# Wider products for retention's keys and values and for gated values with attention's keys and values

## The chip, the cores and the metric

The kernel runs on one core of one Trainium2 chip. The time is the device time of one execution in microseconds (us). Before the change the median of three runs is 982.75 us (982.4 to 984.82). One execution was profiled: it took 980.64 us.

The engines go by the profile's names: PE is the matrix engine (PEld its weight loads), DVE the vector engine, ACT the scalar engine, POOL the GpSimd engine, SP the engine that issues most DMAs.

## The reference, cut to what matters

Two layers of width 1024 over a sequence of 1024. Each layer normalises its input, multiplies it by one wide matrix, splits the result among three groups of heads, and multiplies their outputs by a second matrix:

```python
h = rms_norm(x, pre_gain) * (1.0 + scale) + shift
proj = h @ w_in                       # 1024 x 3088
(aq, ak, av, ag, rq, rk, rv, rg, gq, gk, gv, gg, ga) = jnp.split(proj, IN_SPLITS, axis=-1)
a_out = sliding_window_attention(rotary(aq), rotary(ak), av, sinks) * silu(ag)
r_out = rms_norm(retention(rotary(rq), rotary(rk), rv)) * silu(rg)
g_out = rms_norm(gated_linear_attention(gq, gk, gv, log_a(ga))) * silu(gg)
y = concatenate([a_out, r_out, g_out]) @ w_out
x = x + gate * rms_norm(y, post_gain)
```

Retention's queries, keys, values and gate (rq, rk, rv, rg) have 256 columns each; so have gated attention's values and gate (gv, gg), its queries and keys together (gqk), and attention's keys and values together (kv). Attention's queries and gate have 512 each.

## The kernel before

**Products.** A number is held as two parts, a high and a low one (fp32r), so a product of h with a weight unit takes three passes (high x high, low x high, high x low) over the 8 blocks of 128 rows: 24 matmuls into one bank of PSUM (`accum`). In `project` the stationary operand is a tile of h (128 positions of the sequence) and the moving one is a weight unit of 256 columns (272 for gg, with ga): the result has positions on partitions. In `project_T` and `project_P` it is the other way round: 128 columns of weights are stationary and positions stream, 512 (half of the sequence, from two places, joined by `both`) or 256 (a pair of tiles). The output projection (`y_half`) already streams two weight units joined by `both`, 512 columns in one matmul.

The tag "mm" has three PSUM banks for products (`mm()`, MMB = 3), the other five ("aux") are for the work of cores. A product of 256 columns uses half of a bank.

**Weights.** A weight unit is 256 columns of w_in (or w_out). It is loaded in four pieces of 256 KB into staging tiles ("st", five of them, issued on SP), and each piece is split into its two parts in one of seven places ("arena"): high parts by DVE for the first piece and by ACT for the rest, low parts by DVE and for the last piece by POOL. `PLACE` says which unit goes to which place in which layer, `load` requests a unit as soon as the unit ahead of it in its place has had its last product. `SW` gives places for the last layer's output weights.

**The order on PE** is written out at build time. `layer` runs the products one after another: the two gates (gg, rg), retention (`ret_q` for queries, `project` for keys and values), then `do_gqk`, `do_gv` and `do_kv`, then attention's queries (`attn_rot`) and gates, then the output projection. Everything else is a job, a generator that sleeps for an estimated latency (the table L, in us; a key with "@1" holds for layer 1) on a modelled clock `clk`, which each matmul advances by its columns / 2400 us. `pump` inserts jobs that are due; it is called in `accum` after every 7 matmuls, or every 4 where the result is written as two parts (`len(dst.shape)` of 3), and after each product. PE runs exactly the order so made, and waits where an operand is late. The order on the other engines comes from a scheduler.

**Retention.** `ret_q` for a pair of tiles p makes two products (c = 0, 1) of 256 positions in the two halves of one bank; DVE reads the bank five times (lines 1284 to 1291) and adds (1295). `ret_k` rotates a tile's keys by five operations of DVE (`rotary`, lines 944 to 949), values are multiplied by a decay (line 1658). `ret_core` is the job of one tile: it sleeps rc1, transposes the keys, awaits the queries, sleeps rc2, makes scores, sleeps rc3, then makes the output and carries the state stR to the next tile. A pair's order is: queries, keys of two tiles, values of two tiles; a core is created with the values.

**Gated attention and attention's keys.** `gla_core` (one job for a pair) needs queries, keys and the values of two tiles; `attn_kv` (one job for a tile) rotates and transposes attention's keys. `do_gv` and `do_kv` make their products separately.

The jobs of the gates are `gla_logits` and `gla_log`. The modulation of later stages (`mod_third`) runs as a job beside all this: DVE accumulates 16 tiles of 256 KB a third, each fetched by a DMA (line 317).

## Time and profile before

| what | value |
|---|---|
| median of 3 runs | 982.75 us |
| profiled execution | 980.64 us |
| its span, first to last instruction | 978.5 us |
| granted PE clock | 0.996 |
| matmuls | 7228 |
| of them 128x256 of "mm" with two arena operands | 2304 |
| DMA | 150.34 MB, mean 154 GB/s |

Stages by the order of PE's instructions: preparation and first gate product to 47 us, gates to 88 us, retention of layer 0 to 177 us, gated attention and attention's keys to 285 us, attention's queries and gates and the output projection to 512 us; in layer 1 gates to 562 us, retention to 652 us, gated attention and attention's keys to 757 us, the rest to the end.

A row of a group has line, engine, operation, output<-input, shape and count, then busy time in us, mean duration in ns, and the idle time ahead of it with what ended it. A row of instructions in order of time has start and duration in us. PE's matmuls overlap, so the duration of one is longer than the distance between two starts.

### The profile page before, as it was taken

Reading aid. Unit: us, or ns where it says so; the run is one execution under the profiler, and the core shown is the slowest. Engines: PE = TensorE matmul, PEld = TensorE weight load, DVE = VectorE, ACT = ScalarE, POOL = GpSimd, SP = SyncE. Lnnn points to the kernel's source line nnn. Section 1 sums busy time; section 2 is a strip of 40 time slices with the busy share of each in tenths; the row PEclk is TensorE's granted clock in tenths of the full one; section 3 lists DMA queues with packets and bytes.
Section 4 is the critical chain, followed back from the end, with each engine's and each line's share of the span. In section 5 each row is a group of like instructions: output and inputs, shape, how many; then the busy total and the mean of one; then the engine's idle time right before and its main releaser. Section 6 shows DMA issues by size and latency. Waiting matters only on the chain.

```text
span 978.5 us, 19647 instructions
## 1 busy us (share of the span) xinstructions
PE 958.2 (98%) x7228; PEld 825.8 (84%) x7228; DVE 678.2 (69%) x1598; ACT 395.6 (40%) x1112; POOL 247.7 (25%) x311
## 2 busy tenths in 40 slices
PE   7999999999999999999999999999999999999996
PEld 5799999889998777778889999988999877777875
DVE  6586768678675877645696466785765577677885
ACT  4674102233323656623355420133333257664231
POOL 3431111323310425410133100123332034544000
PEclk9999999999999999999999999999999999999998
DMA  9856315443243345587564121342132434389783
GB/s 353 295 176 197 114 42 150 134 125 103 88 119 118 119 148 184 167 279 242 203 230 152 60 87 33 119 150 62 63 97 77 129 92 135 108 265 282 246 281 121
DMA packets 107532, 150.34 MB, mean 154 GB/s; under 512 B 11142, under 2 KB 58536, under 8 KB 106412
## 3 DMA queue, kind: packets, MB, share of 16 engines
q1 hardware_dynamic: 96140, 134.75, 43.8%
q10 hardware_dynamic: 11296, 14.34, 4.1%
q8 instruction: 57, 0.93, 0.4%
q14 instruction: 39, 0.32, 0.1%
HBM read 110.25 MB, written 36.70 MB: 150 GB/s over the span
## 4 chain that ended last, share of the span: by engine, by line
PE 89%; DVE 6%; DMA 1%; POOL 1%; issue 1%; ACT 1%; SPq 0%; POOLq 0%; DVEq 0%; ACTq 0%
PE mm L170 67%; PE aux L170 18%; PE aux L185 4%; POOL sm L606 1%; DMA ms<-in_w_mod_dram 1%; DMA t<-in_x_dram 0%; DVE t L1288 0%; DVE t L1290 0%; SPq L866 0%; PE mm L185 0%; DVE t L1179 0%; POOL mx L1211 0%; DVE acc L317 0%; DVE t L1099 0%; DVE t L1291 0%
## 5 line engine op out<-in xcount | busy, mean ns | idle before, releaser
L170 PE MATMUL mm<-arena,arena 128*128 128x256 f32 (+2 forms) x1824 | 298.2, 316 | 2.7 <-DVE arena L156 1.4
L170 PE MATMUL mm<-arena 128*128 128x256 f32 (+2 forms) x1728 | 284.7, 318 | 0.0
L170 PEld LDWEIGHTS mm<-arena,arena 128*128 128x128 f32 x1824 | 252.6, 189 | 28.0 <-issue 7.9
L170 PEld LDWEIGHTS mm<-arena 128*128 128x128 f32 x1728 | 240.3, 189 | 24.3 <-issue 4.2
L606 POOL TENSOR_TENSOR sm<-sm,mhalf 128x1 f32<-128x1 f32 (+1 forms) x64 | 57.7, 901 | 292.6 <-DVE sm L603 153.8
L170 PE MATMUL mm<-arena,mx 128*128 128x512 f32 (+1 forms) x564 | 130.9, 388 | 0.0
L170 PEld LDWEIGHTS mm<-arena,mx 128*128 128x128 f32 x564 | 101.5, 188 | 24.0 <-issue 2.3
L154 ACT ACTIVATE t<-aux 128x256 f32<-128x256 f32 (+2 forms) x124 | 52.4, 438 | 97.3 <-PE aux L185 84.6
L154 ACT ACTIVATE arena<-st 128x512 fp32r<-128x512 f32 x94 | 56.1, 628 | 49.4 <-PE mm L170 20.3
L498 POOL TENSOR_TENSOR arena<-st,arena 128x512 fp32r<-128x512 f32 x32 | 45.7, 1429 | 97.5 <-ACT arena L154 81.1
L1049 POOL TENSOR_TENSOR smx<-smx,sm 128x512 f32<-128x512 f32 x32 | 35.0, 1094 | 124.8 <-DVE sm L1048 110.6
L498 DVE TENSOR_TENSOR arena<-st,arena 128x512 fp32r<-128x512 f32 x76 | 59.2, 799 | 3.1 <-ACT arena L154 1.6
L1045 ACT ACTIVATE smx<-smx,sm 128x129 f32<-128x129 f32 x128 | 49.9, 392 | 27.5 <-DVE sm L1042 27.3
L317 DVE SCALAR_TENSOR_TENSOR acc<-ms,c_act,acc 128x512 f32<-128x512 f32 x60 | 45.0, 749 | 17.1 <-DMA ms<-in_w_mod_dram 16.6
L1093 ACT ACTIVATE t<-aux 128x256 f32<-128x256 f32 x32 | 12.3, 383 | 77.3 <-PE aux L170 73.8
L170 PEld LDWEIGHTS aux<-t,mx 32*128 32x128 f32 (+1 forms) x896 | 39.8, 187 | 3.8 <-issue 1.7
L170 PE MATMUL aux<-t,mx 32*128 32x32 f32 (+1 forms) x896 | 40.9, 272 | 0.0
L1040 DVE COPY_PREDICATED smx<-c_masks,aux 128x256 f32<-128x256 int32 x64 | 25.3, 446 | 17.9 <-ACT smx L154 14.5
L1395 DVE SCALAR_TENSOR_TENSOR t<-t,sm,t 128x512 f32<-128x512 f32 x32 | 24.2, 780 | 18.4 <-DMA t<-in_x_dram 12.3
L185 PE MATMUL aux<-c_early,t 128*128 128x128 f32 x186 | 33.8, 277 | 1.5 <-ACT t L1225 0.9
L170 PEld LDWEIGHTS aux<-kT,mx 64*128 64x128 f32 x384 | 24.6, 185 | 10.9 <-issue 7.1
L1098 DVE TENSOR_TENSOR t<-aux,sm 128x256 f32<-128x256 f32 x32 | 13.6, 424 | 27.4 <-POOL sm L606 27.4
(264 smaller groups left out, 1426.9 us busy)
## 6 DMA issues: line engine op xcount, KB each, us to landing
st<-in_w_in_dram SPq DMA_DIRECT2D x96, 256.0 KB, 3.8
ms<-in_w_mod_dram SPq DMA_DIRECT2D x64, 256.0 KB, 3.7
mx<-mixS SPq DMA_DIRECT2D x20, 512.0 KB, 5.6
st<-in_w_last_dram SPq DMA_DIRECT2D x36, 256.0 KB, 3.3
wm<-in_w_m_dram SPq DMA_DIRECT2D x8, 1024.0 KB, 16.7
mixS<-t SPq DMA_DIRECT2D x40, 128.0 KB, 2.1
t<-in_x_dram SPq DMA_DIRECT2D x18, 256.0 KB, 5.0
mixS<-t ACTq DMA_DIRECT2D x32, 128.0 KB, 2.1
```

The source lines that it names most:

```text
L154: A.activation(dst, src, AF.Copy)
L170: T.matmul(dst, lhsT, rhs, start=start, stop=stop)
L185: T.transpose(dst, src, idn)
L317: V.scalar_tensor_tensor(acc, wt, c_act[:, k:k + 1], acc, ALU.mult, ALU.add)
L498: e.tensor_tensor(lo, st, f(hi), ALU.subtract)
L606: G.tensor_tensor(r, r, mhalf[:, :w], ALU.pow)
L1040: V.copy_predicated(sv, curmask.unsqueeze(1).to_broadcast((P, 2, P)), pv[:, :, n // P - 1, :])
L1045: A.activation(sm[:, h, :], sm[:, h, :], AF.Exp, bias=mx[:, h:h + 1], accum_out=sums[:, h:h + 1])
L1049: eng("pn").tensor_tensor(sm[:, :, 0:128], sm[:, :, 0:128], rs.unsqueeze(2).to_broadcast((P, 4, P)), ALU.mult)
L1093: A.activation(sq, po, AF.Square)
L1098: V.tensor_tensor(h4(g1), h4(po), r.unsqueeze(2).to_broadcast((P, 4, 64)), ALU.mult)
L1395: V.scalar_tensor_tensor(xt[j], yg[j], r, xt[j], ALU.mult, ALU.add)
```

## The change

1. Retention's keys and values of a tile become one product: a new `project_2` streams both weight units (512 columns) past the stationary tile of h. The core of a tile is created right after it, and its first sleep, rc1, is 4.5 in both layers (0.8 and 0.0 before).
2. Gated values and attention's keys and values of a tile become one product in the same way (`do_gvkv`).
3. Retention's queries are made by halves of the sequence with `project_T`, two products of 512 positions per half, each with its own bank; `project_P` goes.
4. Units that are streamed together have to lie in places of one arena, so `PLACE` and `SW` change, and with them the order of loads: rk is loaded early where rq was, rq after gg, rv after rg; gqk after the second half's queries; gv and kv together after retention; aq1 after the last of the joint products; the output units o2 and o3, and in the last layer W00 against ag1, change their order.
5. The gates' order: the last pair of gg one place earlier in both layers.

```diff
-SW = dict(W00=6, T1=3, W11=4, W10=5, T2=2, T3=0, T4=1)
+SW = dict(W00=5, T1=3, W11=4, W10=6, T2=2, T3=0, T4=1)
...
-    PLACE.append(dict(gg=_w, rg=5, rq=6, rk=_w, rv=5, gqk=6, gv=_w, kv=5, aq0=6, aq1=_w, ag0=5, ag1=_w,
+    PLACE.append(dict(gg=_w, rg=6, rk=5, rq=_w, rv=6, gqk=_w, gv=5, kv=6, aq0=_w, aq1=5, ag0=6, ag1=_w,
...
+    def project_2(pm, l, t, w0, w1):
+        await_flag(("hT", l, t))
+        c = slice((t % 2) * P, (t % 2) * P + P)
+        h = hT[(l, t // 2)]
+        accum(pm.rearrange("p (s n) -> p s n", s=2), lambda a, k: h[:, a, k, c],
+              lambda b, k: both(w0[:, b, k, 0:256], w1[:, b, k, 0:256]))
...
+    def ret_q(l, hf, w):
+        rqT[hf] = gp.tile([P, NT * P], F32, tag=f"kT{hf}", name=nm("rq"), bufs=1)
+        sn, cs = (tab[:, i, 512 * hf:512 * hf + 512] for i in range(2))
         for c in range(2):
+            pm = mm()
+            project_T(pm, l, hf, w, c * P)
+            u, x = t2(), t2()
+            for b in range(4):
...
+            V.tensor_tensor(u, pm, cs, ALU.mult)
+            V.tensor_tensor(rqT[hf][:, 512 * c:512 * c + 512], u, x, ALU.add)
+            pump()
...
-                load(l, "rk" if name == "gg" else "rv")
+                load(l, "rq" if name == "gg" else "rv")
...
-            for name, p in (("rg", 0), ("rg", 1), ("gg", 2), ("rg", 2), ("gg", 3), ("rg", 3)):
+            for name, p in (("rg", 0), ("rg", 1), ("gg", 2), ("gg", 3), ("rg", 2), ("rg", 3)):
                 do_gates(name, p)
                 if name == "rg" and p == 0:
-                    load(l, "rq")
+                    load(l, "rk")
         else:
-            for ps_ in ((0, 1, 2), (3,)):
-                for name in ("gg", "rg"):
-                    for p in ps_:
-                        do_gates(name, p)
+            for name, ps_ in (("gg", (0, 1, 2)), ("rg", (0, 1)), ("gg", (3,)), ("rg", (2, 3))):
+                for p in ps_:
+                    do_gates(name, p)
...
+        for t in range(NT):
+            if t % 4 == 0:
+                ret_q(l, t // 4, used(l, "rq"))
+                if t:
+                    load(l, "gqk")
+            pm = mm()
+            project_2(pm, l, t, used(l, "rk"), used(l, "rv"))
+            k = ret_k(t, pm[:, 0:256])
+            v = t1()
+            V.tensor_tensor(h4(v), h4(pm[:, 256:512]), vdec.unsqueeze(2).to_broadcast((P, 4, 64)), ALU.mult)
+            job(ret_core(l, t, k, v))
             pump()
...
+        load(l, "gv")
+        load(l, "kv")
...
+        def do_gvkv(p):
+            if p == 0:
+                new_kv()
             for t in (2 * p, 2 * p + 1):
                 pm = mm()
-                project(pm[:, 0:256], l, t, used(l, "gv"))
+                project_2(pm, l, t, used(l, "gv"), used(l, "kv"))
                 vs[t] = t1()
                 copy("gv", vs[t], pm[:, 0:256])
                 if t % 2:
                     job(gla_core(l, p, qks[p], (vs[t - 1], vs[t])))
...
+                job(attn_kv(l, t, pm[:, 256:512]))
                 pump()
 
         do_gqk(0, 0)
         do_gqk(0, 1)
-        do_gv(0)
         do_gqk(1, 0)
-        do_gv(1)
+        do_gvkv(0)
         do_gqk(1, 1)
-        do_gv(2)
-        do_kv(0)
-        do_gv(3)
         for p in range(1, NP_):
-            do_kv(p)
+            do_gvkv(p)
+        load(l, "aq1")
         load(l, "ag0")
...
-                        load(l, ("o3", "ag1")[g])
+                        load(l, ("ag1", "o2")[g])
...
-                        load(l, "o2")
+                        load(l, "o3")
...
-        load(l + 1, "rq")
+        load(l + 1, "rk")
```

More of the change, by code (lines that the diff above doesn't have):

```diff
@@ L594, in project_T @@
               lambda b, k: both(h0[:, b, k, :], h1[:, b, k, :]))
-    def project_P(pm, l, p, w, c):
-        h = hT[(l, p)]
-        accum(pm, lambda a, k: w[:, a, k, c:c + P], lambda b, k: h[:, b, k, 0:256])
+    def project_2(pm, l, t, w0, w1):
[4 more added lines that the diff above has]
+              lambda b, k: both(w0[:, b, k, 0:256], w1[:, b, k, 0:256]))
     def rstd_of(ss, w, scale, eps):
@@ L1271, in gla_out @@
         yield from head_norm_gate(l, t, po, gate, 1.0 / 64.0, EPS, 6)
-    def ret_q(l, p, w):
-        pm = mm()
+    def ret_q(l, hf, w):
+        rqT[hf] = gp.tile([P, NT * P], F32, tag=f"kT{hf}", name=nm("rq"), bufs=1)
+        sn, cs = (tab[:, i, 512 * hf:512 * hf + 512] for i in range(2))
         for c in range(2):
-            project_P(pm[:, 256 * c:256 * c + 256], l, p, w, c * P)
-        def two(x):
-            return x.rearrange("p (c n) -> p c n", c=2)
-        sn, cs = (tab[:, i, 256 * p:256 * p + 256].unsqueeze(1).to_broadcast((P, 2, 256)) for i in range(2))
-        u, x = t2(), t2()
-        for b in range(4):
-            r = slice(32 * b, 32 * b + 32)
-            o = two(x)[32 * (b ^ 1):32 * (b ^ 1) + 32]
-            if b % 2:
-                V.scalar_tensor_tensor(o, two(pm)[r], -1.0, sn[r], ALU.mult, ALU.mult)
-            else:
-                V.tensor_tensor(o, two(pm)[r], sn[r], ALU.mult)
-        V.tensor_tensor(two(u), two(pm), cs, ALU.mult)
-        if p % 2 == 0:
-            rqT[0] = gp.tile([P, NT * P], F32, tag=f"kT{p // 2}", name=nm("rq"), bufs=1)
-        q = rqT[0][:, 512 * (p % 2):512 * (p % 2) + 512]
-        V.tensor_tensor(q, u, x, ALU.add)
-        flag(("rq", l, p), L["rq1"])
-        return two(q)
-    rqT = [None]
+            pm = mm()
+            project_T(pm, l, hf, w, c * P)
+            u, x = t2(), t2()
+            for b in range(4):
+                r = slice(32 * b, 32 * b + 32)
+                o = x[32 * (b ^ 1):32 * (b ^ 1) + 32]
+                if b % 2:
+                    V.scalar_tensor_tensor(o, pm[r], -1.0, sn[r], ALU.mult, ALU.mult)
+                else:
+                    V.tensor_tensor(o, pm[r], sn[r], ALU.mult)
+            V.tensor_tensor(u, pm, cs, ALU.mult)
+            V.tensor_tensor(rqT[hf][:, 512 * c:512 * c + 512], u, x, ALU.add)
+            pump()
+        for p in (2 * hf, 2 * hf + 1):
+            flag(("rq", l, p), L["rq1"])
+    rqT = [None, None]
     def ret_k(t, src):
@@ L1304, in ret_k, with ret_core @@
         return r
-    def ret_core(l, t, q, k, v):
+    def ret_core(l, t, k, v):
         yield lat("rc1", l)
@@ L1314, in ret_core @@
         yield (0.0, ("rq", l, t // 2))
-        qT = q[:, :, P * (t % 2):P * (t % 2) + P]
+        qT = rqT[t // 4].rearrange("p (c n) -> p c n", c=2)[:, :, P * (t % 4):P * (t % 4) + P]
         yield lat("rc2", l)
@@ L1641, in layer @@
         await_flag("tab")
-        for p in range(NP_):
-            last = p == NP_ - 1
-            q = ret_q(l, p, used(l, "rq"))
-            pump()
-            if last:
-                load(l, "gqk")
-            ks = {}
-            for name in ("rk", "rv"):
-                w = used(l, name)
-                for tt in range(2):
-                    t = 2 * p + tt
-                    pm = mm()
-                    project(pm[:, 0:256], l, t, w)
-                    src = pm[:, 0:256]
-                    if name == "rv":
-                        v = t1()
-                        V.tensor_tensor(h4(v), h4(src), vdec.unsqueeze(2).to_broadcast((P, 4, 64)), ALU.mult)
-                        job(ret_core(l, t, q, ks[tt], v))
-                    else:
-                        ks[tt] = ret_k(t, src)
-                    pump()
-                if last:
-                    load(l, {"rk": "gv", "rv": "kv"}[name])
+        for t in range(NT):
[9 more added lines that the diff above has]
+            job(ret_core(l, t, k, v))
+            pump()
+        load(l, "gv")
+        load(l, "kv")
         G.memset(stC, 0.0)
@@ L1683, in do_gqk @@
                 load(l, "aq0")
-        def do_gv(p):
+        def do_gvkv(p):
+            if p == 0:
+                new_kv()
             for t in (2 * p, 2 * p + 1):
                 pm = mm()
-                project(pm[:, 0:256], l, t, used(l, "gv"))
+                project_2(pm, l, t, used(l, "gv"), used(l, "kv"))
                 vs[t] = t1()
@@ L1692, in do_gv @@
                     job(gla_core(l, p, qks[p], (vs[t - 1], vs[t])))
-                pump()
-            if p == NP_ - 1:
-                load(l, "aq1")
-        def do_kv(p):
-            if p == 0:
-                new_kv()
-            for t in (2 * p, 2 * p + 1):
-                pk = mm()
-                project(pk[:, 0:256], l, t, used(l, "kv"))
-                job(attn_kv(l, t, pk))
+                job(attn_kv(l, t, pm[:, 256:512]))
                 pump()
@@ L1756, in layer @@
                 if hf:
-                    if l == DEPTH - 1 and g == 0:
+                    if l == DEPTH - 1 and g:
                         sw_first("W00")
                     else:
-                        load(l, ("o3", "ag1")[g])
+                        load(l, ("ag1", "o2")[g])
         for hf in range(2):
@@ L1827 @@
 EN = {"shw0": "V", "shw1": "A", "shw2": "A", "shw3": "A", "slw0": "V", "slw1": "G", "slw2": "V", "slw3": "G", "sht2": "A", "sht3": "A", "sht4": "A", "slt2": "V", "slt3": "G", "slt4": "G", "sd": "V", "mh0": "A", "mh1": "A", "mh2": "A", "mh3": "A", "mf": "A", "ms0": "V", "ms1": "V", "ms2": "V", "ms3": "V", "yg0": "V", "yg1": "V", "ml0": "V", "ml1": "V", "ml2": "V", "ml3": "V", "mod0": "A", "mod1": "V", "qst": "S", "smh": "A", "sml": "S", "sm0": "S", "sm1": "S", "lao": "S", "sao": "S", "lmix": "S", "ssg": "S", "lsg": "S", "ssr": "S", "lsr": "S", "lx": "S", "sx": "A", "lw": "S", "lwm": "S", "whi0": "V", "whi1": "A", "whi2": "A", "whi3": "A", "wlo0": "V", "wlo1": "V", "wlo2": "V", "wlo3": "G", "xn0": "V", "xn1": "V", "hlo0": "V", "hlo1": "V", "rot0": "V", "rot1": "V", "rdec": "V", "kslo": "V", "qslo": "V", "vlo": "G", "kT": "A", "qT": "A", "sprev": "A", "pn": "G", "pf0": "A", "aoc": "A", "hng": "V", "mh": "A", "gso": "V", "mg": "V", "mgl": "V", "rT": "A", "rv": "A", "gv": "A", "gk": "A", "ak0": "V", "ak1": "V", "ak2": "V", "ak3": "V", "kd0": "G", "kd1": "G", "kd2": "G", "kx1": "G", "kx2": "G", "kx3": "V", "kx4": "V", "qb": "G", "stx": "V"}
-L = {"tt6": 3.0, "sw1": 0.45, "ld1": 1.34, "ld2": 1.2, "ld1@1": 1.35, "ld2@1": 1.31, "swW00": 0.0, "swT1": 0.0, "swW11": 0.34, "swW10": 0.4, "tt1": 16.0, "tt2": 1.62, "tt3": 0.84, "tt4": 1.15, "rq1": 6.5, "pf3": 3.0, "pf4@2": 4.2, "pf4@3": 7.0, "pf5": 0.9, "mod1": 4.6, "mod2": 3.86, "mod3": 12.15, "mod4": 6.79, "mod5": 3.18, "mod6": 9.21, "pre1": 7.44, "kv1": 3.56, "kv2": 5.4, "aq1": 6.0, "aq7": 6.12, "ag1": 6.23, "aq2": 2.4, "aq6": 5.2, "aq3": 10.48, "aq4": 7.36, "aq5": 4.92, "hn1": 8.56, "hn2": 2.85, "gz1": 10.94, "gz2": 9.73, "gl1": 2.76, "gd3": 16.72, "gc1": 0.81, "gc2": 1.64, "gc3": 1.94, "gc4": 1.17, "gc6": 1.32, "gc5": 1.06, "rc1": 0.8, "rc2": 2.64, "rc3": 5.87, "rc4": 4.72, "fin1": 6.58, "lay1": 1.0, "gc4@1": 1.09, "mod2@1": 4.0, "mod3@1": 15.1, "mod5@1": 3.36, "mod6@1": 4.11, "pre1@1": 7.83, "kv1@1": 3.37, "kv2@1": 5.28, "aq1@1": 4.66, "aq7@1": 5.28, "ag1@1": 7.05, "aq2@1": 0.82, "aq6@1": 6.35, "aq3@1": 11.11, "aq4@1": 5.23, "aq5@1": 5.22, "hn1@1": 7.81, "hn2@1": 2.85, "gz1@1": 13.93, "gz2@1": 10.64, "gl1@1": 4.6, "gd3@1": 15.9, "gc1@1": 0.31, "gc2@1": 1.94, "gc3@1": 1.33, "gc6@1": 0.86, "gc5@1": 0.94, "rc1@1": 0.0, "rc2@1": 0.87, "rc3@1": 2.72, "rc4@1": 2.98, "fin1@1": 4.28, "lay1@1": 1.54}
@@ new lines @@
+L = {"tt6": 3.0, "sw1": 0.45, "ld1": 1.34, "ld2": 1.2, "ld1@1": 1.35, "ld2@1": 1.31, "swW00": 0.0, "swT1": 0.0, "swW11": 0.34, "swW10": 0.4, "tt1": 16.0, "tt2": 1.62, "tt3": 0.84, "tt4": 1.15, "rq1": 6.5, "pf3": 3.0, "pf4@2": 4.2, "pf4@3": 7.0, "pf5": 0.9, "mod1": 4.6, "mod2": 3.86, "mod3": 12.15, "mod4": 6.79, "mod5": 3.18, "mod6": 9.21, "pre1": 7.44, "kv1": 3.56, "kv2": 5.4, "aq1": 6.0, "aq7": 6.12, "ag1": 6.23, "aq2": 2.4, "aq6": 5.2, "aq3": 10.48, "aq4": 7.36, "aq5": 4.92, "hn1": 8.56, "hn2": 2.85, "gz1": 10.94, "gz2": 9.73, "gl1": 2.76, "gd3": 16.72, "gc1": 0.81, "gc2": 1.64, "gc3": 1.94, "gc4": 1.17, "gc6": 1.32, "gc5": 1.06, "rc1": 4.5, "rc2": 2.64, "rc3": 5.87, "rc4": 4.72, "fin1": 6.58, "lay1": 1.0, "gc4@1": 1.09, "mod2@1": 4.0, "mod3@1": 15.1, "mod5@1": 3.36, "mod6@1": 4.11, "pre1@1": 7.83, "kv1@1": 3.37, "kv2@1": 5.28, "aq1@1": 4.66, "aq7@1": 5.28, "ag1@1": 7.05, "aq2@1": 0.82, "aq6@1": 6.35, "aq3@1": 11.11, "aq4@1": 5.23, "aq5@1": 5.22, "hn1@1": 7.81, "hn2@1": 2.85, "gz1@1": 13.93, "gz2@1": 10.64, "gl1@1": 4.6, "gd3@1": 15.9, "gc1@1": 0.31, "gc2@1": 1.94, "gc3@1": 1.33, "gc6@1": 0.86, "gc5@1": 0.94, "rc1@1": 4.5, "rc2@1": 0.87, "rc3@1": 2.72, "rc4@1": 2.98, "fin1@1": 4.28, "lay1@1": 1.54}
```

## The prediction

> **What bounds the kernel now.** I read the page first (busy time, clock, the chain that ended last), then what PE waited for, then its groups by shape, then its instructions in order of time at the places that the change touches.

> ```profile
> span 978.5 us, 19647 instructions
> PE 958.2 (98%) x7228; PEld 825.8 (84%) x7228; DVE 678.2 (69%) x1598; ACT 395.6 (40%) x1112; POOL 247.7 (25%) x311
> PEclk9999999999999999999999999999999999999998
> PE 89%; DVE 6%; DMA 1%; POOL 1%; issue 1%; ACT 1%; SPq 0%; POOLq 0%; DVEq 0%; ACTq 0%
> ```

> PE is busy throughout at the full granted clock, and 89% of the chain that ended last is PE. The next view says that almost nothing stops it. It lists what PE's matmuls waited for (total us, times, longest):

> ```profile
> PE mm L170 <- DVE arena L156: 1.4, 1, 1.4
> PE mm L170 <- DVE t L1291: 1.3, 1, 1.3
> ...
> PE aux L185 <- ACT t L1225: 0.9, 2, 0.5
> ```

> The first two lie in the retention stage, the third in gated attention; the other waits of PE are under 0.7 us in sum there, or lie in the first 61 us, ahead of anything that changes. So the time is the length of PE's stream: how many matmuls at what spacing, plus the few waits. The change must act on one of these two.

> **The stream: what is removed and added.** The groups by shape give the counts (times, mean ns):

> ```profile
> L170 PE MATMUL mm<-arena,arena 128*128 128x256 f32 x1152 | 150.6, 285 | 2.7 <-DVE arena L156 1.4 <-DVE t L1291 1.3
> L170 PE MATMUL mm<-arena 128*128 128x256 f32 x1152 | 150.1, 285 | 0.0
> L170 PE MATMUL mm<-arena,arena 128*128 128x512 f32 x480 | 122.3, 402 | 0.0
> L170 PE MATMUL mm<-arena 128*128 128x512 f32 x480 | 122.1, 401 | 0.0
> ```

> A product is 24 matmuls (3 passes over 8 blocks). Per layer, retention's queries are 4 x 2 products of 256 columns, its keys and values 8 tiles x 2, gated values and attention's keys and values 8 x 2: 40 products. In two layers that is 80 x 24 = 1920 of the 2304 matmuls of 128x256; the other 384 are the retention gates (8 x 24 x 2). They become 960 matmuls of 128x512. The streamed columns stay the same, 1920 x 256; 960 matmuls and 960 weight loads go. The means of 285 and 401 ns are no price, since matmuls overlap. The price is the distance between starts in a stretch that nothing interrupts:

> ```profile
> 544.11 5.77 PE L170 MATMUL mm<-arena,arena 128*128 128x256 f32 x48
> 549.72 3.16 PE L170 MATMUL mm<-arena 128*128 128x272 f32 x24
> 552.71 0.39 PE L170 MATMUL aux<-gaT,gwt 128*128 128x512 f32 x1
> ...
> 556.16 5.91 PE L170 MATMUL mm<-arena,arena 128*128 128x256 f32 x48
> 561.91 5.92 PE L170 MATMUL mm<-arena 128*128 128x256 f32 x48
> 567.67 0.99 PE L170 MATMUL mm<-arena,arena 128*128 128x256 f32 x7
> ```

> Start to start, 48 matmuls of 256 columns took 5.61, 5.75 and 5.76 us: 116.9, 119.8 and 120.0 ns each. The third stretch is a product of retention's queries. For 512 columns the nearest rows are pieces of the chain (start, us) of the output projection, which has the new form (weights of two places streamed past a stationary tile), and of attention's queries, which have the form that retention's queries get; then two rows of the last layer:

> ```profile
> 480.71 11.15 PE mm L170 x48
> ```

> ```profile
> 761.51 15.64 PE mm L170 x68
> ```

> ```profile
> 942.80 5.76 PE L170 MATMUL mm<-arena,mx 128*128 128x512 f32 x24
> 948.40 2.96 PE L170 MATMUL mm<-arena,a 128*128 128x512 f32 x12
> ```

> These are 232.3, 230.0 and (5.60 us for 24) 233.3 ns. Two narrow matmuls against one wide one:

> - queries: 192 pairs (2 layers x 4 x 24) x (240.0 - 230.0) = **1.9 us** saved;
> - the rest: 768 pairs x (2 x 118.35, the middle of 116.9 and 119.8, - 232.3 = 4.4 ns) = **3.4 us** saved.

> Sum: 5.3 us. The ends are 960 x (2 x 116.9 - 233.3 = 0.5 ns) = 0.5 us and 960 x (240.0 - 230.0) = 9.6 us. A loss is excluded by these rows: no pair of narrow rows is faster than a wide one. The saving isn't the weight load: a narrow matmul of 272 columns (2.99 us for 24, 124.6 ns) is some 5 to 8 ns dearer than one of 256, so columns set the spacing and not the load, and what goes is a fixed part per matmul.

> The jobs that run between the matmuls (cores of retention and of gated attention) keep their instructions and their number of insertions; I take the cost of an insertion as the same between wide and narrow matmuls. The chunk between two chances to insert a job was 7 x 0.12 = 0.84 us and becomes 4 x 0.232 = 0.93 us: nothing.

> **Waits that go.** The 1.3 us wait is at 645 us: the third of layer 1's last four key and value products needs the bank that the last product of queries left, and DVE reads that bank late.

> ```profile
> 640.39 3.41 PE L170 MATMUL mm<-arena 128*128 128x256 f32 x27
> 645.10 2.75 PE L170 MATMUL mm<-arena,arena 128*128 128x256 f32 x21 [1.29 <-DVE t L1291]
> ```

> ```profile
> 640.13 0.68 DVE L1290 TENSOR_TENSOR t<-mm,tab 32x512 f32<-32x512 f32 x1
> ...
> 644.26 0.69 DVE L1291 TENSOR_TENSOR t<-mm,tab 128x512 f32<-128x512 f32 x1
> ...
> 647.70 0.28 DVE L949 TENSOR_TENSOR t<-t,tr 128x128 f32<-128x128 f32 x1
> ```

> With three banks in turn, a narrow product (24 x 0.119 = 2.9 us) comes back to a bank after two others, 5.7 us later; a wide one after 11.1 us. DVE's five reads of the queries' bank took 640.13 to 644.95, so 11.1 us cover them: -1.3 us. The 1.4 us wait is at 101.4 us, for the values' weights: requested when the last gate product ends at 88.2, issued at 89.68, converted by DVE at 100.88, behind DVE's work on the queries.

> ```profile
> 89.68 1.87 SPq L159 DMA_DIRECT2D st<-in_w_in_dram x4
> ...
> 100.88 0.41 DVE L156 CAST arena<-st 128x512 fp32r<-128x512 f32 x1
> ```

> Now they are needed 48 x 0.231 = 11.1 us after 88.2, at 99.3, as early as before (a narrow query product, two key products), but DVE has the time between the queries' two halves for the conversion. I count half: -0.7. Together -2.0 us; ends 0 and -2.7.

> **What moves and is covered.** DVE, ACT and POOL keep their instructions and shapes (six operations of 512 columns per query product, 0.69 us each by the rows above); DMAs keep their number on SP, in another order. The second gate's last tiles run one pair earlier in both layers. In layer 0 they would start at 70.28, and DVE writes the last remainders of their input until 70.36; remainders are first read in the second pass, 8 x 0.125 = 1 us after the start:

> ```profile
> 69.08 1.28 DVE L692 TENSOR_TENSOR arena<-t,arena 128x512 fp32r<-128x512 f32 x2
> 70.28 0.99 PE L170 MATMUL mm<-arena 128*128 128x256 f32 x7
> ```

> So 0, at worst 1 us. Gated values' and attention's key weights are now requested together after the last retention tile and needed three wide products later, 72 x 0.232 = 16.7 us and the jobs between. In the old order the two units were converted between these rows, 168.23 to 185.01 (16.8 us, some 8.4 a unit):

> ```profile
> 168.23 1.15 ACT L154 ACTIVATE arena<-st 128x512 fp32r<-128x512 f32 x2 [2.71 <-PE mm L170]
> ```

> ```profile
> 183.72 1.29 POOL L498 TENSOR_TENSOR arena<-st,arena 128x512 fp32r<-128x512 f32 x1 [7.18 <-ACT arena L154]
> ```

> The last retention cores run there too, so the jobs make the difference; and DVE, the converter, has room by these windows (us; busy of PE, PEld, DVE, ACT, POOL) of retention in layers 0 and 1, where it is busy for 74%:

> ```profile
> 88.20:177.40 89.20, 87.78 (x748) 85.49 (x747) 66.40 (x165) 16.85 (x36) 12.41 (x10) 1.00 0.37 114
> 561.90:652.30 90.40, 89.11 (x759) 86.63 (x757) 66.93 (x166) 18.85 (x42) 11.04 (x10) 1.00 0.28 87
> ```

> I cost it at nothing. Gated cores end later by some 16 us (three products of keys no longer stand behind them) and fill attention's query products, where PE had no job at all (the piece of 68 above). Attention's second query unit is requested two wide products, 11.1 us, before its use; at 8.4 us a unit it arrives.

> **The wait that is added.** Keys and values of a tile now come from one product, so the key's rotation on DVE starts as its core is created; before, the key was two narrow products (5.7 us) old. The core therefore sleeps 4.5 us of the planner's time instead of 0.8 (0 in layer 1). The planner counts 213 ns for a wide matmul that takes 232, so this is 4.9 us. Behind a key's late transpose stands all of PE. In the old layer 1 a key product ended at 640.8 (3 matmuls into the row at 640.39 above) and its rotation at 648.0 (the row at 647.70); the next product ended 24 x 0.119 later, at 643.6, its rotation five operations later, some 1.1 us, at 649.1: 7.2 and 5.5 us. These stood directly behind a burst of queries; in the new order one whole product (5.6 us) lies between, but two query products follow each other, 8.2 us of DVE work (12 x 0.69) in 11.1 us beside the rest. Ends: -0.9 us (the small wait of gated attention above goes, where products are longer) and 4 bursts x (2.3 + 0.6) = +11.6 us. I take **+2.0**: one late burst in four (2.9) less the 0.9, nearest to the windows' DVE share of 74%.

> **Sum.** -5.3 - 2.0 + 2.0 = -5.3 us. The profiled execution took 980.64 us, its span 978.5: 975.3 for it. The median shown is 982.75: **977.4 us**, 0.54% less. About 0.3% (2.9 us) is what a measurement can tell from no change.

> **Rivals.**

> 1. *The fixed part is small* (0.20). If the new products take 233.3 ns and the old ones were of the 116.9 kind, the saving is 0.5 us: 982.75 - 0.5 - 2.0 + 2.0 = 982.2 us, no change. For it: rows of both kinds exist and new weights come from two places. Against it: the queries' own row is 120.0. [...]
> 2. *DVE becomes late for the keys* (0.15). Place: the key transposes at the head of each half; price 11.6 us in place of 2.0; it decides from the point where product end to rotated key takes over 4.9 us. 982.75 - 5.3 - 2.0 + 11.6 = 987.0 us, slower. For it: 7.2 us were seen, and DVE waits in order for weights of the modulation, as the row below shows. Against: the product that now lies between.
> 3. *All goes well* (0.13): stream near its upper end, both waits and the small ones gone: 982.75 - 7.1 - 2.7 - 0.9 = 972.0 us.

> ```profile
> DVE acc L317 <- DMA ms<-in_w_mod_dram: 16.6, 14, 3.6
> ```

> **Numbers.** The forecast has 0.52. Faster: 0.52 + 0.13, less 0.03 for its edge above 979.8: 0.62. Slower: 0.13 (rival 2 less 0.02 that stay under 985.7). Within 0.3%: 0.25. The range takes in the forecast, rival 1, most of rival 3 and half of rival 2: 972 to 986.

> **What would show it.** 128x256 groups of PE at 384 in all and 128x512 groups of the two arena kinds at 1920; uninterrupted new products at 230 to 233 ns a matmul; no wait on the query reads; DVE's and ACT's counts as before; waits of transposes on keys (DVE L949) short or absent. New PE waits over 3 us at the first tiles of a half, or on the loads at the first gated value product, would make the prediction wrong; so would a spacing over 236.

## The result and the profile after

The changed kernel took **994.23 us** (989.79 to 1003.26, four runs) beside 982.58 us (981.52 to 984.82) of the kernel before, run beside it: a ratio of 1.0139 with a 95% interval of 1.0095 to 1.0183. It is slower by 11.7 us where 5.3 us less were forecast. In the profiled execution it took 990.48 us. Four lines of its page: span, busy time, granted clock in 40 slices, and engines of the chain that ended last.

```profile
span 988.7 us, 17715 instructions
...
PE 959.6 (97%) x6268; PEld 778.4 (79%) x6268; DVE 676.7 (68%) x1598; ACT 395.6 (40%) x1112; POOL 245.0 (25%) x311
...
PEclk9999999999999999999999999999999999999998
...
PE 84%; DVE 8%; DMA 3%; issue 2%; POOL 2%; ACT 1%; SPq 1%; POOLq 0%; DVEq 0%; ACTq 0%
```

The span is 10.2 us longer. PE has 960 matmuls fewer, as planned; DVE and ACT have the counts and the busy time of before. But the chain is 84% PE where it was 89%, and DVE's share rose from 6% to 8%: PE now waits. The groups by shape:

```profile
L170 PE MATMUL mm<-arena,arena 128*128 128x512 f32 x960 | 246.2, 406 | 1.8 <-DVE arena L156 1.8
L170 PE MATMUL mm<-arena 128*128 128x512 f32 x960 | 243.5, 402 | 0.0
...
L170 PE MATMUL mm<-arena,arena 128*128 128x256 f32 x192 | 24.7, 284 | 0.0
L170 PE MATMUL mm<-arena 128*128 128x256 f32 x192 | 23.9, 285 | 0.0
```

These are the counts that the prediction named (1920 wide, 384 narrow). What PE's matmuls waited for (us in total, times, longest):

```profile
PE aux L185 <- DVE mx L1244: 3.1, 2, 1.6
PE aux L170 <- DVE t L1089: 2.5, 2, 1.4
PE mm L170 <- DVE arena L156: 1.8, 1, 1.8
...
PE mm L170 <- DMA a<-mixS: 1.4, 1, 1.4
...
PE aux L185 <- ACT t L1228: 1.2, 2, 0.7
PE aux L185 <- DVE t L952: 1.0, 1, 1.0
PE aux L185 <- DVE t L639: 1.0, 1, 1.0
```

In the changed kernel L1244 copies gated scores out of their banks, L1089 splits a finished head's output, L952 ends a key's rotation, L1228 copies gated keys. All waits of this view, its small rows too, sum to 21.3 us, against 12.7 before. The waits on L1244, L1089, L1228 and L952, 7.8 us, all lie in the stage of the **joint products** of gated values with attention's keys and values (200 to 300 and 680 to 790 us). Before, the same four places come to 1.5 us: the 0.9 on L1225 that the prediction shows (L1228 here), and

```profile
PE aux L185 <- DVE mx L1241: 0.6, 2, 0.4
```

which is L1244 here. Nothing of the rise was in the prediction. The wait on the query reads is gone, as forecast; that for the values' weights is 1.8 us in place of 1.4.

One such place, PE in order of time (start, us):

```profile
239.13 0.38 PE L185 MATMUL aux<-c_early,mx 128*128 128x128 f32 x2
239.45 0.42 PE L170 MATMUL aux<-t,mx 32*128 32x32 f32 x6
241.23 1.41 PE L170 MATMUL aux<-t,mx 32*128 32x32 f32 x41 [1.36 <-DVE t L1089]
...
242.90 1.13 PE L185 MATMUL aux<-c_early,t 128*128 128x128 f32 x3
243.68 3.32 PE L170 MATMUL mm<-arena 128*128 128x512 f32 x8
246.93 1.54 PE L170 MATMUL aux<-t,mx 32*128 32x32 f32 x48
```

A gated core transposes (one small bank) and then makes a burst of scores into four more, all five "aux" banks. The burst stops after six of its rows (three matmuls of the kernel, one bank each: the 28 matmuls of a burst show as 56 rows, 48 and 8), because the fourth bank it wants is still to be read by DVE at L1089. That bank holds a finished head's transposed output; ACT's copy of it, which L1089 needs, was over at 238.79:

```profile
238.41 0.38 ACT L154 ACTIVATE t<-aux 128x256 fp32r<-128x256 f32 x1 [1.48 <-PE aux L185]
```

DVE's side of it:

```profile
238.04 0.21 DVE L952 TENSOR_TENSOR t<-t,tr 128x64 f32<-128x64 f32 x1
238.18 0.28 DVE L1170 TENSOR_SCALAR t<-t 128x256 f32<-128x256 f32 x1
238.50 0.69 DVE L1172 TENSOR_TENSOR_SCAN t<-c_late,t 128x256 f32<-128x256 f32 x1
239.22 0.22 DVE L1176 SCALAR_TENSOR_TENSOR mid<-t,t 128x32 f32<-128x32 f32 x1
239.47 0.42 DVE L1177 TENSOR_TENSOR t<-t,mid 128x256 f32<-128x256 f32 x1
239.81 1.03 DVE L1182 TENSOR_TENSOR t<-mid,t 128x64 f32<-128x64 f32 x4
240.75 0.42 DVE L1089 TENSOR_TENSOR t<-aux,t 128x256 fp32r<-128x256 f32 x1
```

DVE kept to the order of its program here: the rotation of a key is over at 238.25, but then the decays of the next pair (L1170 to L1182, 238.18 to 240.8) stand ahead of the one short operation that frees the bank, which starts 1.96 us after its operand is there.

The eight wide matmuls at 243.68 took 3.32 us in place of 2.1 (2.08 at 255.00). The view by windows says why (window, length, busy of PE, PEld, DVE, ACT, POOL with counts, granted clock, DMA):

```profile
239.52:242.93 3.41, 2.05 (x57) 1.90 (x57) 3.41 (x10) 1.44 (x4) 0.00 (x0) 1.00 0.23 77
242.93:246.35 3.42, 3.42 (x10) 2.51 (x10) 2.07 (x8) 1.21 (x6) 0.00 (x0) 0.50 0.25 78
246.35:249.76 3.41, 3.41 (x64) 2.80 (x63) 1.37 (x5) 0.68 (x4) 2.03 (x5) 1.00 0.13 42
```

For exactly 3.41 us after the burst the granted clock is 0.50: a **half-clock window**, worth up to 1.7 us (half of its length). Between the first and the last microseconds the kernel before has none; the changed one has three, at 103, 243 and 762 us, each behind one of the waits (101.9, 241.2 and 761.5 us). The forty-slice row of the page doesn't show them, since a slice is 24 us long. The clock record of this profile has the two values 0.50 and 1.00 alone. Between the first and the last microseconds its three stretches at 0.50 are 3.41 us long each, and those at 1.00 between them are multiples of that: 136.53 us (40) and 515.41 us (151). Inside the three, wide matmuls mostly start 426 to 427 ns apart; at full clock the median is 232.

**The account** of the span: waits +8.6 us (21.3 - 12.7), half clock +5.1 (10.24 us at half), which leaves -3.5 for everything else; together +10.2. The next sections test each of the three.

### The profile page after: what moved, and what is told of

Same layout as the page of the kernel before. It is cut to its first block, busy times and chain, and to the rows that moved or that the text cites. A ratio compares the mean times of both kernels' runs of the same rounds, so it can differ in the third digit from the quotient of the medians.

```text
span 988.7 us, 17715 instructions
## 1 busy us (share of the span) xinstructions
PE 959.6 (97%) x6268; PEld 778.4 (79%) x6268; DVE 676.7 (68%) x1598; ACT 395.6 (40%) x1112; POOL 245.0 (25%) x311
## 4 chain that ended last, share of the span: by engine, by line
PE 84%; DVE 8%; DMA 3%; issue 2%; POOL 2%; ACT 1%; SPq 1%; POOLq 0%; DVEq 0%; ACTq 0%
PE mm L170 63%; PE aux L170 16%; PE aux L185 4%; POOL sm L609 1%; DMA st<-in_w_last_dram 1%; DMA t<-mixF 1%; DVE t L1490 1%; DVE arena L498 1%; DMA t<-in_x_dram 1%; DVE mx L1424 0%; DVE t L1393 0%; DVE t L1495 0%; SPq L869 0%; DVE t L1182 0%; PE mm L185 0%
## 5 line engine op out<-in xcount | busy, mean ns | idle before, releaser
L170 PE MATMUL mm<-arena,arena 128*128 128x512 f32 (+2 forms) x1344 | 296.4, 372 | 1.8 <-DVE arena L156 1.8
L170 PE MATMUL mm<-arena 128*128 128x512 f32 (+2 forms) x1248 | 279.7, 375 | 0.0
L170 PEld LDWEIGHTS mm<-arena,arena 128*128 128x128 f32 x1344 | 224.4, 190 | 46.0 <-issue 5.0
L170 PEld LDWEIGHTS mm<-arena 128*128 128x128 f32 x1248 | 211.3, 190 | 41.3 <-issue 3.9
L170 PE MATMUL mm<-arena,mx 128*128 128x512 f32 (+1 forms) x564 | 131.0, 388 | 0.7 <-DVE t L1490 0.6
L170 PEld LDWEIGHTS mm<-arena,mx 128*128 128x128 f32 x564 | 101.4, 188 | 25.2 <-issue 1.9
L154 ACT ACTIVATE t<-aux 128x256 f32<-128x256 f32 (+2 forms) x124 | 52.0, 435 | 102.5 <-PE aux L185 87.4
L154 ACT ACTIVATE arena<-st 128x512 fp32r<-128x512 f32 x94 | 56.1, 627 | 58.7 <-PE mm L170 30.3
L498 DVE TENSOR_TENSOR arena<-st,arena 128x512 fp32r<-128x512 f32 x76 | 63.1, 857 | 2.0 <-PE mm L170 1.5
L498 POOL TENSOR_TENSOR arena<-st,arena 128x512 fp32r<-128x512 f32 x32 | 45.1, 1409 | 71.3 <-ACT arena L154 54.9
L1096 ACT ACTIVATE t<-aux 128x256 f32<-128x256 f32 x32 | 12.3, 384 | 104.9 <-PE aux L170 104.9
L317 DVE SCALAR_TENSOR_TENSOR acc<-ms,c_act,acc 128x512 f32<-128x512 f32 x60 | 45.2, 753 | 10.3 <-DMA ms<-in_w_mod_dram 9.4
L170 PEld LDWEIGHTS aux<-t,mx 32*128 32x128 f32 (+1 forms) x896 | 40.8, 187 | 7.1 <-issue 2.8
L170 PE MATMUL aux<-t,mx 32*128 32x32 f32 (+1 forms) x896 | 42.0, 272 | 2.5 <-DVE t L1089 2.5
L185 PE MATMUL aux<-c_early,t 128*128 128x128 f32 (+1 forms) x186 | 34.0, 279 | 6.3 <-DVE mx L1244 3.1
L185 PEld LDWEIGHTS aux<-c_early,t 128*128 128x128 f32 (+1 forms) x186 | 24.0, 142 | 15.5 <-DVE mx L1244 4.3
L1101 DVE TENSOR_TENSOR t<-aux,sm 128x256 f32<-128x256 f32 x32 | 13.6, 425 | 29.8 <-POOL sm L609 29.8
L1043 DVE COPY_PREDICATED smx<-c_masks,aux 128x256 f32<-128x256 int32 x64 | 25.2, 446 | 11.6 <-ACT smx L154 11.3
```

Of the source, the lines that this page charges most:

```text
L154: A.activation(dst, src, AF.Copy)
L170: T.matmul(dst, lhsT, rhs, start=start, stop=stop)
L185: T.transpose(dst, src, idn)
L317: V.scalar_tensor_tensor(acc, wt, c_act[:, k:k + 1], acc, ALU.mult, ALU.add)
L498: e.tensor_tensor(lo, st, f(hi), ALU.subtract)
L1043: V.copy_predicated(sv, curmask.unsqueeze(1).to_broadcast((P, 2, P)), pv[:, :, n // P - 1, :])
```

## The experiments

The runs were made in five groups, each with runs of the kernel before beside it, with medians of 981.32, 979.88, 981.2, 981.55 and 981.88 us. A ratio is to those. Theory A puts the loss into the joint stage, theory B into retention.

**The changed kernel once more, unedited.**

> The changed kernel once more, beside the runs below. Both theories: about 994 us at the median, runs from 989 to 1004, and the spread is the granted clock: a run's span goes with its share of half clock (0.991 at 988.7 us, 0.978 at 1001.5 us).

994.21 us (990.33 to 1001.44), ratio 1.0135 (1.0101 to 1.0169). Its six runs go roughly with the granted clock: 990.33 at 0.991, 997.68 at 0.984, 996.89 at 0.980, 1001.44 at 0.978. Beside them the kernel before spreads by 6 us, this one by 11.

**Retention's part alone**; gated values and attention's keys as before, in the old order.

```diff
-                project_2(pm, l, t, used(l, "gv"), used(l, "kv"))
+                project(pm[:, 0:256], l, t, used(l, "gv"))
...
+                project(pk[:, 0:256], l, t, used(l, "kv"))
+                job(attn_kv(l, t, pk))
```

> Retention's part of the change alone: gated values and attention's keys are separate products again, in the old order. Theory A (the cost comes from the joint products: attention's key transposes and the gated cores ask for the same banks at the same time, PE waits, and the waits set off half-clock stretches): about 980 us (982.6, less 1.9 and 1.7 us of spacing, less the 1.3 us wait, plus some 2 us for the late value weights with a half-clock stretch), and no waits on lines 1089 and 1244. Theory B (the cost comes from retention, whose keys are transposed too early): 988 us or more.

983.07 us, ratio 1.0012 (0.9998 to 1.0025). Theory B falls. It is 3 us above theory A's figure, and the waits on L1089 and L1244 didn't go but are small, 0.8 and 0.6 us, the former with a half-clock window behind it (679.5 us).

**The joint stage alone**; retention as before.

```diff
-def ret_core(l, t, k, v):
+def ret_core(l, t, q, k, v):
...
-"rc1": 4.5
+"rc1": 0.8
```

> The joint products of gated values and attention's keys alone: retention by pairs of tiles, with separate keys and values and its old sleeps. Theory A: 988 to 993 us, with the waits on lines 1089 and 1244 as in the changed kernel. Theory B: 979 to 983 us.

1000.11 us, ratio 1.0202 (1.0168 to 1.0236): more than the whole loss. PE waits 3.7 us on the score copies and has five half-clock stretches, 20.5 us in sum. That is 7 us above theory A's range; why the joint stage loses more alone than together with the new retention isn't shown. Theory A holds for the place; the next runs look for the mechanism.

**Keys transposed later.**

```diff
-"kv1": 3.56, "kv1@1": 3.37
+"kv1": 9.0, "kv1@1": 9.0
```

> The changed kernel with attention's key transposes 9 us of the planner's time after their product instead of 3.4 to 3.6, which puts them behind the gated core's two bursts of scores. Theory A: the waits on line 1244 (3.1 us) and on line 952 (1.0 us) go, and with them one or more half-clock stretches of 1.7 us: 984 to 989 us. Theory B: no change from the changed kernel, 990 us or more.

1005.47 us, ratio 1.0251 (1.0219 to 1.0282): a miss. The wait on L952 went and that on L1244 fell to 0.3 us, and score bursts waited instead, 3.9 us in two places, for the bank that a late transpose held (the key split L963). So time for the rotation isn't what is short.

**Key transposes in a product bank** (by the prediction's estimate a wide product comes back to its bank after 11.1 us, a narrow one after 5.7, so the product banks have room).

```diff
     yield lat("kv1", l)
-    pt = aux()
+    pt = mm()
```

> The changed kernel, but the transposed attention keys go to one of the three product banks instead of one of the five small banks. Theory A2 (the five small banks are what is contended: a gated core's score burst needs all five, and each key transpose holds one of them until DVE and ACT have split it): the waits of the transposes on DVE L1244 (3.1 us) go, no wait of the same size takes their place, and with them at least one of the half-clock windows; 985 to 990 us. Rival D (DVE is late in the joint stage, whichever bank it frees): waits of the same size appear on the product banks or on the score bursts (DVE L1089, L952); 993 to 1000 us.

991.56 us, ratio 1.0102 (1.0073 to 1.0131): a part, between the ranges of A2 (the banks) and D (DVE late, whichever bank it frees). Two lines of PE's waits:

```profile
PE aux L170 <- DVE t L1089: 2.5, 2, 1.4
...
PE aux L170 <- DVE mx L1244: 0.4, 1, 0.4
```

L1244 fell from 3.1 to 0.4; the burst's own wait on the fifth bank is as it was, and so are three half-clock windows.

**Longer sleeps ahead of the bursts**, and then both edits.

```diff
-"gc2": 1.64, "gc2@1": 1.94, "gc3": 1.94, "gc3@1": 1.33
+"gc2": 3.6, "gc2@1": 3.6, "gc3": 3.6, "gc3@1": 3.6
```

> The changed kernel, with the gated core's two sleeps ahead of its score bursts raised from 1.64/1.94 and 1.94/1.33 us to 3.6 us in both layers, which gives DVE more time before each burst. Rival D: the waits of the joint stage (DVE L1244, L1089; 5.6 us together) fall below 2 us, 985 to 990 us. Theory A2: the bursts move, the banks are as contended; waits of 4 us or more stay in the stage, 991 to 998 us.

> Both of the former edits. If banks and DVE's time each carry a part, waits of the joint stage under 1 us, no half-clock window in it, and 981 to 985 us; under A2 alone as the first of the two (985 to 990), under D alone as the second (985 to 990).

1014.0 us (ratio 1.034, 1.0319 to 1.0361) and 1010.78 us (1.0302, 1.0281 to 1.0322): both miss. The waits only changed lines (L963, L1228, L1101, L1189), 31.7 and 29.2 us in all, with eight half-clock stretches in each. More time for DVE didn't help here, where the banks were held longer.

**When half clock follows: waits of known length** added to the kernel before.

```diff
+    def probe(n):
+        pa = aux()
+        for i in range(4):
+            transp(pa[:, i * P:(i + 1) * P], ident, ident)
+        y = [mod_stage(), mod_stage()]
+        A.activation(y[0], pa, AF.Copy)
+        for i in range(n):
+            A.activation(y[(i + 1) % 2], y[i % 2], AF.Copy)
+        pb = aux()
+        transp(pb[:, 0:P], y[n % 2][:, 0:P], ident)
...
+            if not hf:
+                probe((2, 3, 4, 5, 1, 6, 3, 8)[4 * l + 2 * g + c])
```

> The kernel before with work added: after each of the eight query products of attention's first half, PE makes four transposes, ACT copies 512 columns 2 to 9 times (about 0.6 us each), and PE then transposes the last copy, so that PE stands still for a known time in the middle of wide matmuls. Theory H1 (a half-clock stretch of 3.41 us follows every wait above some length): the longest waits are followed by matmuls of 427 ns, the shortest are not, and the order gives the length. Theory H2 (it takes a stretch in which PE does narrow work and waits; a lone wait of up to 5 us among wide matmuls does nothing): no wait, or only those near 5 us, is followed by such a stretch. About 982 us plus 25 us of waits, plus 1.7 us for each stretch.

The eight waits came to between 1.35 and 7.11 us. The two shortest:

```profile
292.37 0.33 PE L185 MATMUL aux<-c_early,ms 128*128 128x128 f32 x1 [2.01 <-ACT ms L987]
292.45 7.34 PE L170 MATMUL mm<-arena,arena 128*128 128x512 f32 x24
...
788.00 0.33 PE L185 MATMUL aux<-c_early,ms 128*128 128x128 f32 x1 [1.35 <-ACT ms L987]
788.09 5.74 PE L170 MATMUL mm<-arena 128*128 128x512 f32 x24
```

After 2.01 us the 24 matmuls take 7.34 us, after 1.35 us the usual 5.74. All seven waits from 2.01 us on are followed by half clock, the one of 1.35 isn't. H1 held for lone waits. But in the changed kernel the burst at 239 us waited for 1.36 us and half clock followed, so the length of a wait alone doesn't tell these cases apart.

**Narrow work without a wait**, added to the kernel before.

```diff
+    def probe(n):
+        pa = aux()
+        for i in range(n):
+            transp_n(pa[:, 16 * (i % 32):16 * (i % 32) + 16])
+
+    def transp_n(dst):
+        mult(dst, ident, ident[:, 0:16], True, True, 0.125)
...
+                probe((12, 16, 20, 24, 28, 32, 40, 56)[4 * l + 2 * g + c])
```

> The kernel before with work added: after each of the eight query products of attention's first half, PE makes 12, 16, 20, 24 (layer 0), 28, 32, 40 and 56 matmuls of 16 columns in a row (about 0.125 us each, 1.5 to 7 us), and waits for nothing. Theory H3 (what counts is the columns that PE streams in a fixed window of 3.41 us; under about a third of the window, the next one runs at half the clock): the long lumps (24 and more, 3 us and more) are followed by half-clock windows though PE never waits, the short ones are not. Theory H1 (a wait sets it off): none is followed by one. Time about 982 plus 28 us, plus 1.7 us for each window.

Each of these matmuls shows as two in the trace (24 rows for 12, 32 for 16), so the lumps are twice as long as planned (2.75 us and more). Two lumps and what follows them, then the windows at the second:

```profile
293.06 2.75 PE L170 MATMUL aux<-c_early 128*128 128x16 f32 x24
295.65 5.79 PE L170 MATMUL mm<-arena,arena 128*128 128x512 f32 x24
301.28 3.64 PE L170 MATMUL aux<-c_early 128*128 128x16 f32 x32
304.77 7.37 PE L170 MATMUL mm<-arena 128*128 128x512 f32 x24
```

```profile
301.46:304.87 3.41, 3.41 (x32) 3.41 (x33) 2.49 (x4) 1.23 (x2) 0.00 (x0) 1.00 0.24 93
304.87:308.28 3.41, 3.41 (x10) 2.64 (x10) 0.00 (x0) 0.86 (x2) 0.00 (x0) 0.50 0.34 77
```

| columns in a window | windows | followed by half clock |
|---|---|---|
| under 2,050 | 34 | 34 |
| 2,050 to 2,540 | 12 | 11 |
| 2,540 to 3,110 | 35 | 24 |
| 3,110 to 3,770 | 49 | 13 |
| more | 4,912 | 1 |

The window of 239.52 us above has 1,820, that of the second lump about 1,000. The kernel before comes down to 3,590 at its lowest (277 us), inside the band in which 13 of 49 were followed by half clock: it had little margin.

**The joint products spread** as gated values were before.

```diff
-        do_gqk(1, 0)
         do_gvkv(0)
+        do_gqk(1, 0)
+        do_gvkv(1)
         do_gqk(1, 1)
-        for p in range(1, NP_):
-            do_gvkv(p)
+        do_gvkv(2)
+        do_gvkv(3)
```

> The changed kernel with its joint products in the places that gated values had before (two query and key products of the second half between them), so that the gated cores start 22, 22 and 11 us of products apart instead of 22, 11 and 11. Theory R (cores follow each other too closely for the banks and for DVE): waits of the joint stage from some 8 us to under 4, one half-clock window less, 985 to 990 us. Rival A2 (the two kinds of jobs meet wherever they stand): 992 to 997 us, as the changed kernel. A late weight load at the first joint product would add 2 to 5 us.

1005.57 us, ratio 1.023 (1.0199 to 1.0262), above the ranges of both: the waits on L1089 alone are 4.0 us, and theory R falls. The jobs meet wherever they stand, as A2 says, but why this order is 11 us worse isn't shown.

**Bursts in two halves**, two banks at a time, and that with two more edits.

```diff
-            sp = [aux() for _ in range(4)]
...
+            for hs in ((0, 1), (2, 3)):
+                sp = {h: aux() for h in hs}
...
+                if hs[0] == 0:
+                    yield 0.1
```

> The changed kernel with each score burst of the gated core made in two halves of two heads, two banks each, with wide matmuls between the halves. If bank demand (five of five) and the long narrow stretch are the cause (A2 with H3): waits of transposes and bursts in the joint stage under 3 us together, no half-clock window in that stage, and 981 to 986 us. If DVE's time is the cause (D): waits for the same DVE lines stay, 990 us or more.

> The changed kernel with the two former edits, and with the second half's gate logarithms started 6 us later, so that they don't stand ahead of the value weights' conversion at 100 us. If each cause is named rightly: no half-clock window after the start, waits as in the kernel before (about 4 us in the stages that change), and the saving of the stream of some 5 us left: 975 to 980 us. If not: 985 us or more.

1044.59 us (ratio 1.0633, 1.0592 to 1.0675) and 1049.85 us (1.0677, 1.0631 to 1.0724). A miss with a reason, in the first one's trace:

```profile
224.81 1.53 PE L170 MATMUL aux<-t,mx 32*128 32x32 f32 x24
226.17 0.39 PE L170 MATMUL aux<-t 32*128 32x32 f32 x4
```

Half a burst, on two of the four groups of 32 rows, took as long as a whole one did on all four: 24 rows of the trace in 1.53 us, where 48 took 1.54 (shown above). The waits on L1244 and L1089 are gone, as A2 said, but the narrow stretches doubled, and half-clock time outside the ends rose to 82 us, 41 us lost. For the clock this is H3 once more; the edit itself is no test of the price of the banks. The last run's gate logarithms, 6 us later, left the weights' wait at 1.9 us.

**A spare bank.** The core's transposes go to a product bank too, so that a burst takes four of five; and the first piece of layer 0's value weights is converted on ACT.

```diff
     yield lat("kv1", l)
-    pt = aux()
+    pt = mm()
...
     yield lat("gc2", l)
-    pt = aux()
+    pt = mm()
...
-                if first:
+                if first or name == "rv" and l == 0:
                     A.activation(hi, st, AF.Copy)
```

> The changed kernel with both kinds of jobs of the joint stage moved off the small banks by one bank each (the key transposes and the gated core's key transposes go to product banks), so that a score burst of four banks finds a fifth one spare; and with the first conversion of the value weights of layer 0 on ACT, where it doesn't stand behind the query rotation on DVE. Theory A2 (a burst that needs five of five banks stops for whichever DVE is late with): the waits on DVE L1089 (2.5 us) and L1244 go; the weights' wait of 1.8 us falls below 0.7; with them at least two of the three half-clock windows; 981 to 986 us. Theory D (DVE is late for the burst's operands too, behind the decays of the next pair): the bursts wait on other lines of DVE for as long; 989 to 993 us.

**980.76 us** (979.88 to 984.12), ratio 0.9993 (0.9979 to 1.0007): 13.5 us gone. The weights' wait fell to 1.0 us, on ACT now (L494), and not below 0.7 as expected. With the two bank edits alone:

> The changed kernel with the two bank edits alone, the value weights left as they were: splits the 13.5 us of the three edits together. From the traces the weights' share is 0.8 us of wait and 1.7 us of half clock; so 982 to 984.5 us if the banks are the larger part, 987 or more if not.

981.96 us, ratio 0.9997 (0.9984 to 1.001). So the banks are 12.3 of the 13.5 us; the rest, the weights' share, is inside the intervals. All waits of PE in its joint stages:

```profile
PE mm L185 <- DVE t L952: 1.0, 1, 1.0
PE aux L170 <- DVE mx L1244: 0.4, 1, 0.4
```

7.8 us became 1.4, though DVE has the same work to do, and no half-clock window is left there; the one at 102 us is the weights'. (The kernel of 980.76 us has the same two waits and one window, at 262.8 us; the weights' is gone.) Theory A2, the banks, holds; D, that DVE's time is short whichever bank it frees, falls.

**The control: the kernel before with the same three edits.**

> The kernel before with the same three edits as the kernel that took 980.76 us (both transposes in product banks, the value weights of layer 0 converted on ACT): a control. If the edits mend what the change broke (A2), they are worth little here: the before trace has 0.9 + 0.6 us of waits on the small banks and 1.4 us for the weights, so 978 to 981.5 us. If they are simply good for any kernel of this kind, and the change still loses its 13 us: 965 to 972 us.

**979.5 us**, ratio 0.9974 (0.9957 to 0.999): 2.4 us here against 13.5 there. The edits mend what the change broke; and this is the lowest median of the study, clear of the kernel before, though not of the 980.76 us (the intervals overlap). So even with the banks mended the wider products show no gain: the span of that kernel is 978.3 us beside the control's 976.7, its waits 14.7 us beside 10.4 (the weights, the joint stage, layer 1's first gates and the last output, 1.0, 1.4, 1.0 and 2.3 us), and its half-clock window costs 1.7 us more. That is 6.0 us for a span longer by 1.6: what the stream saves, some 4 us in these two executions, is spent there.

**Retention alone with the weight edit**, and **decays on POOL** in the kernel of 980.76 us.

```diff
-"ak0": "V", "ak1": "V"
+"ak0": "G", "ak1": "G"
```

> The retention part alone (as in the second run, 983.07 us), with the same edit for the value weights of layer 0. If that wait and what it does to the clock are all that holds the retention part back: 1.8 us of waits and up to 1.7 us of half clock less, 979.5 to 981.5 us, at or a little under the kernel before (981.3). If its stream saves nothing: 982 to 984 us.

> The kernel that took 980.76 us, with two of the four subtractions in the decays of gated attention on POOL in place of DVE (0.5 us of DVE per pair less, ahead of a score burst). If DVE's queue is what is left of the trouble in layer 0 (waits of 1.0 on L952 and 0.4 on L1244, one half-clock window at 262.8 us): these go, 977 to 979.5 us. If POOL, which is slower, becomes late in its place: 981 to 985 us.

980.56 us, ratio 0.9998 (0.9981 to 1.0016), and 982.08 us, ratio 1.0006 (0.9991 to 1.0021). The retention half, with its late load down to a wait of 1.0 us, is worth nothing that can be measured. With the decays on POOL the waits on L952 and L1244 stay (1.0 and 0.6 us) and three half-clock stretches remain: what is left in layer 0 isn't mended by that, and the time is in the range that was given for POOL becoming late. On the page of the kernel of 980.76 us one operation that both engines run (L498, 128x512) takes 1,383 ns on POOL and 847 ns on DVE.

## Why the prediction was wrong

Point by point, by its own steps:

- **The stream's spacing (-5.3) was right.** Distances between the starts of neighbouring matmuls of products, from 61 us on, waits and half clock left out, are 122.5 ns on average from narrow to narrow (some 2,100 in the kernel before) and 239.2 ns from wide to wide, alike in both kernels; the medians, 119 and 232 ns, are those of the prediction's rows. A pair saves 2 x 122.5 - 239.2 = 5.8 ns; some 910 pairs of steps were changed, 5.3 us.
- **"The cost of an insertion as the same" was wrong, by about 2 us.** The way into a job and back, less one step, is 132 + 83 - 122.5, some 93 ns, between narrow matmuls. For the new wide ones the two kernels' sums differ by nearly 80 ways in of some 255 ns and 80 ways back of some 105 ns: 255 + 105 - 239, some 120 ns. The difference, 25 to 30 ns at some 80 insertions, is 2.0 to 2.4 us. 5.3 less that is about 3, near the -3.5 that the account left over.
- **Waits that go (-2.0).** The one on the query reads went (-1.3). The weights' one grew by 0.4: the conversion stands on DVE behind the second query product's first operations, and those wait for the product. "DVE has the time between the queries' two halves" failed, and in the profiled execution a half-clock window also followed the wait, at 103 us (in that of the unedited repeat the same 1.8 us didn't).
- **The wait that is added (+2.0)** was put at retention's keys. No PE wait on a rotated key lies there; retention's part cost nothing.
- **"What moves and is covered ... I cost it at nothing" is the step that failed.** It asked whether weights arrive and whether DVE has room, by windows with 74% busy, which are of retention; in the gated stage DVE was busy for 69% and 64% in the kernel before. It didn't count the banks: a core and its burst need all five, and a joint product now sets off the key transposes, which take one of them, beside the burst, while a finished head's output may hold another. DVE's mean share said nothing, since one short read (0.42 us) behind 2.6 us of other work held a whole burst. This gave 6.3 us of waits more in that stage (7.8 less the 1.5 that the kernel before has there on the same lines); with 3.2 us of new waits elsewhere it makes the 8.6: 6.3 + 3.2 - 1.3 + 0.4.
- **The half clock was in no step.** With the full clock everywhere in the profile of before, I took it as given. It is 5.1 us in this execution and 13.7 in the profiled one of the unedited repeat (27.3 us at half clock between the ends), and so the runs spread.
- Rival 2 had the right engine but the wrong stage and half the mechanism; its 987.0 us is short of 994. Rival 1 is out: 5.8 ns a pair, not 0.5; and rival 3's 7.1 us wasn't reached.

What stays open: why the joint stage alone loses more than the whole change; what decides for the windows around 3,000 columns (in the profile of the changed kernel half clock followed one of 3,072, not one of 3,008), and where the 3.2 us of waits outside the joint stage come from (1.0 us at layer 1's first gates, 2.0 at the last output; the mended kernel has them too).

## What to carry to other kernels

When two products are joined, their consumers start together: count what they hold at once (here banks, five of five) before you count engine time. In this kernel, which lives on PE's stream, a wait of 1.36 us next to narrow matmuls was dearer than it looks, because half clock followed for 3.41 us, up to 1.7 us more; look for the places with the fewest streamed columns per window (here half clock followed 34 of 34 windows under 2,050 columns, and 1 of 4,912 above 3,770). A spare bank for the burst was worth 12.3 us in the changed kernel, against the some 3 us that the wider products save net of insertions, and with the weight edit 2.4 us in the old one: look for such an edit first.

## What the runs showed that was not expected

- Half clock without any wait: 32 matmuls of 16 columns, PE busy throughout, then 3.41 us at 0.50.
- Narrow matmuls of 32 rows: 48 rows of the trace took 1.54 us over four row groups, 24 took 1.53 us over two.
- Between wide matmuls a job's insertion costs some 120 ns, between narrow ones some 93 ns.
